# Both down projections by seven block products, with the weight sums moved

## The chip, the cores and the metric

The kernel runs on one core of a Trainium2 chip. The core has five engines that run side by side, each with its own queue of instructions in order: TensorE (PE in the profile, its weight loads PEld), VectorE (DVE), ScalarE (ACT), GpSimd (POOL) and SyncE (SP), which issues most of the DMA transfers. Sixteen DMA engines move the data. The metric is the time of one execution on the device in microseconds, lower is better, as the median of several runs.

## The reference

One decoder layer on 512 tokens of width 1024, in float32:

```python
h = swiglu(rms_norm(x, ffn1_pre_norm), ffn1_w_gate, ffn1_w_up, ffn1_w_down)
x = x + 0.5 * rms_norm(h, ffn1_post_norm)
u = rms_norm(x, mix_pre_norm)
# mixer: u @ w_in, three branches (sparse attention, gated delta rule,
# cross-attention into 256 memory tokens), each to width 1024, gated by
# sigmoid(u @ w_branch_gate), summed, then @ w_out
x = x + rms_norm(merged @ w_out, mix_post_norm)
h = swiglu(rms_norm(x, ffn2_pre_norm), ffn2_w_gate, ffn2_w_up, ffn2_w_down)
x = x + 0.5 * rms_norm(h, ffn2_post_norm)

def swiglu(x, w_gate, w_up, w_down):
    return (jax.nn.silu(x @ w_gate) * (x @ w_up)) @ w_down
```

The hidden width of both feed-forward blocks is 2816 = 22 x 128. The two products with `w_down` (512 x 2816 by 2816 x 1024) are what the change is about.

## The kernel before

**Products in three matmuls.** Every float32 operand of a large product is split into a rounded high part and a remainder, hi and lo. ScalarE makes hi (a cast), VectorE or POOL makes lo (a subtraction). A product of a 128-row block is then three matmuls, hi·hi, lo·hi and hi·lo, accumulated in PSUM (`mm3`, lines 115 to 119). Weights come in tiles of 128x512 through `wload` (line 88), from a small ring of buffers: SyncE issues the load of `wraw`, ScalarE casts to `whi`, VectorE subtracts to `wlo`; where `pool_every` is set, every so many-th subtraction goes to POOL instead.

**Stages.** In order of time: first gate and up projections, 22 tiles of 128 hidden features, result in `H` (features by tokens); first down projection; norm, then the input projections, the delta rule and the compression of the mixer; attention (task list `order2`); the gated merge of the branches (task list `order4`); `w_out`; the second gate and up; the second down; the last norm and store.

**Products by seven.** A two-by-two block product can be made with seven block products instead of eight when sums of the blocks of both operands are formed first (Winograd's form of Strassen's scheme). The kernel before does that in four places. From the seventh tile on, both gate and up stages pair the gate and up weights of a tile with two halves of the input (`fast_prods`, line 425; `fast_load` forms the weight sums on VectorE). The gated merge does the same with two gate tiles. And the second down projection does it (`down7`, line 535), with token halves and halves of the hidden features as blocks: 11 feature tiles, two token blocks of 128 and 512 output columns to a product.

The weight sums of `down7` are too large for VectorE. `weight_sums` (line 518) forms them in DRAM, by DMA from POOL: four tensors `T1` to `T4`, each made by a copy and one accumulating transfer, eight transfers in all, each cut into four pieces of 704 KB. A piece is issued after the matmul that was last when the piece was written (`self.order(i, self.mmark, Sync)`): POOL's queue stands until PE has done it. In the kernel before the 32 pieces are for the second down projection (`ffn2_d`), and they are issued beside the *first* gate and up stage, two in each of the sixteen tiles by seven.

**The first down projection before** is the plain one (`down_half`, line 505): for each half of the tokens and each half of the output columns, 22 feature tiles times two token blocks times three matmuls. `hsplit` makes hi and lo of `H`, tile by tile. Around it stands a list of tasks, `order0`: `d0`, `d1` are the two token halves of the projection, `p` its norm and residual (`postnorm`), `n` the next norm, `t` the transposes that give the input of the mixer (`xth`, `xtl`), `k0` to `k3` and `v` the key and value projections of the memory tokens, which depend on nothing here and fill PE while a norm runs. The norm of the memory tokens (`mem_norm`) is made during `d0`.

**What sets the order.** The program is written task by task; a planner then orders the instructions of each engine by priority, which is the place in the program unless a task is moved ahead by its number in `off0`, `off`. An engine never reorders on the chip: an instruction that waits holds up everything behind it on its engine. The plan is by `tasks` and the lists in `PRM`.

**In `down7` before** the seven products come in the order X = first block, Q (`T3`), X again (`T2`), Y, Z (`T1`), X again (`T4`), Z again. X, Y, Z and Q are two PSUM banks each, all eight together. Between them stand copies from bank to bank (X to Y, X to Z), Q to SBUF, and the sums of the output for the last 256 tokens in `c2`. In the last product the last eight feature tiles are done for the first token block, then for the second, so that the ending of the first block runs beside it.

Of the kernel before, what the change touches and what calls it, by code (L numbers as in the profile page):

```python
# [15 lines left out]
OP = mybir.AluOpType  # L16
# [23 lines left out]
class Body:  # L40
    def __init__(self, ctx, tc, a, out, tap):
        self.tc, self.nc, self.a, self.out, self.tap = tc, tc.nc, a, out, tap
        pool = lambda name, **k: ctx.enter_context(tc.tile_pool(name=name, **k))
        self.sp = pool("sp", bufs=2)
        self.cp = pool("cp", bufs=1)
        self.ring, self.ringi = None, 0
        self.nload, self.pool_every = 0, 0
        self.tp = pool("tp", bufs=2)
        self.wp = pool("wp", bufs=1)
        self.wx, self.nx = None, 0  # L50
        self.ps = pool("ps", bufs=1, space=bass.MemoryType.PSUM)
# [18 lines left out]
        self.dmaq = 0  # L70
        self.own = 0


    def bank(self, tag, name):
# [40 lines left out]
    def mm3(self, out, lh, ll, rh, rl, first, last):  # L115
        t = self.nc.tensor
        t.matmul(out, lh, rh, start=first, stop=False)  # L117
        t.matmul(out, ll, rh, start=False, stop=False)  # L118
        self.mmark = t.matmul(out, lh, rl, start=False, stop=last)  # L119
# [299 lines left out]
    def fast_tile(self, f, S, T, banks, s7, H, side=()):  # L419
        g, up = self.fast_prods(S, T, banks, s7, side=side)  # L420
# [4 lines left out]
    def fast_prods(self, S, T, banks, s7, mid=(), side=()):  # L425

        nc, v, te = self.nc, self.nc.vector, self.nc.tensor
        hi, lo = S
        a, q7, g, u = banks
        a, q7, u = a[:, :256], q7[:, :256], u[:, :256]  # L430

        def prod(out, w, t, start=False):
            th, tl = T[t]
            for k in range(4):
                c = slice(k * P, k * P + P)
                wh, wl = hi[:, w, c], lo[:, w, c]
                m = lambda x, y, **kw: te.matmul(out, x, y, skip_group_check=True, **kw)  # L437
                m(wh, th[:, k], start=start and k == 0, stop=False)
                m(wl, th[:, k], start=False, stop=False)
                self.mmark = m(wh, tl[:, k], start=False, stop=k == 3)  # L440
            if side and w in (self.S_S3, self.S_S1):
                side.pop(0)()
# [1322 lines left out]
```

## Time and profile before

| | us |
|---|---|
| median of 3 runs | 1324.87 |
| the three runs | 1321.78, 1324.87, 1331.35 |
| the profiled execution, its own time | 1321.78 |
| its span, first to last instruction | 1320.0 |
| first gate and up, tiles by seven (they overlap the last plain tiles) | 69.6 to 248.5 |
| first down projection with its memory work | 248.5 to about 398 |
| attention | about 640 to 800 |
| gated merge | about 800 to 930 |
| second gate and up, tiles by seven | about 1056 to 1207 |
| second down projection | 1207.4 to 1312.4 |
| ending after the last matmul | 1312.4 to 1320.0 |

The profile is one execution, and the times in its rows are from the start of its span. A row of the windows view gives the length of a stretch, then for each engine how long it was busy in it (and with how many instructions), the clock granted to TensorE as a share of full speed, the mean busy share of the sixteen DMA engines and the GB/s that they moved. A row of a group view gives line, engine, operation, output and inputs with their shapes and count, then total busy time and the mean of one in ns, then how long the engine sat idle just before them and for whom. Matmuls overlap in the pipeline: a matmul's own span is longer than the distance to the next.

### The profile page before, as it was taken

Reading aid. Unit: us, or ns where it says so; the run is one execution under the profiler, and the core shown is the slowest. Engines: PE = TensorE matmul, PEld = TensorE weight load, DVE = VectorE, ACT = ScalarE, POOL = GpSimd, SP = SyncE. Lnnn points to the kernel's source line nnn. Section 1 sums busy time; section 2 is a strip of 40 time slices with the busy share of each in tenths; the row PEclk is TensorE's granted clock in tenths of the full one; section 3 lists DMA queues with packets and bytes.
Section 4 is the critical chain, followed back from the end, with each engine's and each line's share of the span. In section 5 each row is a group of like instructions: output and inputs, shape, how many; then the busy total and the mean of one; then the engine's idle time right before and its main releaser. Section 6 shows DMA issues by size and latency. Waiting matters only on the chain. (4 is left out here: it accounts for less than half of the span.)

```text
span 1320.0 us, 21997 instructions
## 1 busy us (share of the span) xinstructions
PE 1286.8 (97%) x8025; PEld 1118.4 (85%) x8025; DVE 968.8 (73%) x1812; ACT 735.7 (56%) x1532; POOL 151.7 (11%) x145
## 2 busy tenths in 40 slices
PE   9999999999999989999999999999999999999997
PEld 7889999877888778888777778898878899999886
DVE  6898778478575876754779776565699687876977
ACT  7566555476555644323655545543678466664653
POOL 0021111100000321110221112132300000000000
PEclk9999999999999999999999999999999999999999
DMA  7557998877664433241321133232854533323763
GB/s 253 193 184 259 232 239 239 193 247 225 219 207 133 119 104 91 58 144 45 117 65 50 48 106 110 73 97 65 287 165 147 176 113 113 112 82 105 263 206 137
DMA packets 113165, 198.52 MB, mean 150 GB/s; under 512 B 18604, under 2 KB 28192, under 8 KB 113056
## 3 DMA queue, kind: packets, MB, share of 16 engines
q1 hardware_dynamic: 103808, 173.78, 41.3%
q0 software_dynamic: 8960, 23.07, 7.8%
q8 instruction: 63, 1.03, 0.3%
q14 instruction: 46, 0.38, 0.1%
q10 hardware_dynamic: 288, 0.26, 0.1%
HBM read 187.03 MB, written 33.08 MB: 167 GB/s over the span
## 5 line engine op out<-in xcount | busy, mean ns | idle before, releaser
L106 ACT CAST whi<-wraw 128x512 fp32r<-128x512 f32 (+1 forms) x286 | 173.7, 617 | 159.2 <-PE pfm L119 59.7
L109 DVE TENSOR_TENSOR wlo<-wraw,whi 128x512 fp32r<-128x512 f32 (+1 forms) x255 | 174.8, 694 | 74.9 <-ACT whi L106 65.7
L117 PE MATMUL pfm<-xth,whi 128*128 128x512 f32 x272 | 108.0, 402 | 1.0 <-DVE X L1055 0.6
L118 PE MATMUL pfm<-xth,wlo 128*128 128x512 f32 x272 | 108.4, 403 | 0.1
L119 PE MATMUL pfm<-xtl,whi 128*128 128x512 f32 x272 | 107.8, 402 | 0.0
L437 PE MATMUL smm<-thi,fset 128*128 128x256 f32 x384 | 68.9, 278 | 4.3 <-ACT ss L450 4.3
L109 POOL TENSOR_TENSOR wlo<-wraw,whi 128x512 fp32r<-128x512 f32 x28 | 38.0, 1356 | 229.1 <-ACT whi L106 165.0
L437 PEld LDWEIGHTS smm<-thi,fset 128*128 128x128 f32 x384 | 58.3, 188 | 4.8 <-ACT ss L450 4.7
L117 PEld LDWEIGHTS pfm<-xth,whi 128*128 128x128 f32 x272 | 51.0, 189 | 11.6 <-issue 1.8
L459 DVE TENSOR_TENSOR up<-s,smm 128x256 f32<-128x256 f32 x32 | 13.5, 421 | 62.5 <-ACT se L454 62.5
L119 PEld LDWEIGHTS pfm<-xtl,whi 128*128 128x128 f32 x272 | 50.9, 188 | 9.7 <-issue 0.8
L118 PEld LDWEIGHTS pfm<-xth,wlo 128*128 128x128 f32 x272 | 50.9, 188 | 9.2 <-DVE wlo L109 0.5
L437 PE MATMUL smm<-thi,fxtl 128*128 128x256 f32 x192 | 53.5, 279 | 0.6 <-DVE fxtl L412 0.6
L437 PE MATMUL smm<-thi,fxth 128*128 128x256 f32 x192 | 53.4, 278 | 0.2 <-ACT ss L450 0.2
L584 ACT CAST ringh<-ringr 128x1024 fp32r<-128x1024 f32 (+1 forms) x39 | 37.8, 975 | 27.3 <-PE acc_s L597 6.5
L437 PE MATMUL se<-thi,fset 128*128 128x256 f32 x256 | 45.7, 278 | 0.0
L403 DVE TENSOR_TENSOR fs<-fq 128x1024 f32<-128x1024 f32 x32 | 39.0, 1219 | 8.3 <-issue 5.4
L1173 ACT ACTIVATE Pm<-Pm,nm 128x384 f32<-128x384 f32 (+2 forms) x64 | 35.6, 558 | 14.5 <-DVE nm L1172 13.9
L437 PEld LDWEIGHTS se<-thi,fset 128*128 128x128 f32 x256 | 38.8, 188 | 0.0
L437 PEld LDWEIGHTS smm<-thi,fxtl 128*128 128x128 f32 x192 | 36.1, 188 | 1.0 <-DVE fxtl L412 1.0
L409 ACT CAST fset<-fq 128x512 fp32r<-128x512 f32 x48 | 29.6, 620 | 12.5 <-PE ss L437 5.9
L437 PEld LDWEIGHTS smm<-thi,fxth 128*128 128x128 f32 x192 | 36.0, 188 | 0.4 <-ACT ss L450 0.4
(645 smaller groups left out, 4271.7 us busy)
## 6 DMA issues: line engine op xcount, KB each, us to landing
wraw<-in_ffn_d_dram SPq DMA_DIRECT2D x94, 256.0 KB, 2.9
T<-in_ffn_d_dram POOLq DMA_DIRECT2D x24, 704.0 KB, 8.3
fq<-in_ffn_g_dram SPq DMA_DIRECT2D x64, 256.0 KB, 3.0
fq<-in_ffn_u_dram SPq DMA_DIRECT2D x64, 256.0 KB, 3.8
ringr<-T SPq DMA_DIRECT2D x20, 512.0 KB, 4.1
wraw<-in_ffn_g_dram SPq DMA_DIRECT2D x34, 256.0 KB, 3.2
wraw<-in_ffn_u_dram SPq DMA_DIRECT2D x34, 256.0 KB, 3.4
woraw<-in_w_out_dram SPq DMA_DIRECT2D x32, 256.0 KB, 4.2
```

The source lines that it names most:

```text
L106: nc.scalar.copy(hi, raw)
L109: eng.tensor_tensor(lo, raw, hi.bitcast(F32), op=OP.subtract)
L117: t.matmul(out, lh, rh, start=first, stop=False)
L118: t.matmul(out, ll, rh, start=False, stop=False)
L119: self.mmark = t.matmul(out, lh, rl, start=False, stop=last)
L403: add = lambda *x: v.tensor_tensor(*x, op=OP.add)
L409: nc.scalar.copy(hi[:, i], q[:, i])
L437: m = lambda x, y, **kw: te.matmul(out, x, y, skip_group_check=True, **kw)
L459: v.tensor_tensor(up[:, 256:], s7, a, op=OP.subtract)
L584: nc.scalar.copy(hi, raw)
L1173: nc.scalar.activation(pm, pm, AF.Exp, bias=nm[:, qb : qb + 1], scale=-1.0, accum_out=sm[:, qb : qb + 1])
```

## The change

The first down projection is made by `down7` too. Its weight sums take the place of the second one's beside the first gate and up stage, in 8 x 11 = 88 pieces of 256 KB, and the second one's, still in 32 pieces of 704 KB, go beside attention and the gated merge. Pieces are no longer issued at fixed places in a tile but by a count of matmul columns: `tick` is called once per group of three matmuls, adds their columns, and when the sum passes `pace` (4600 and 15000) the next piece is issued, waiting for that matmul. The counting starts at the fourth tile of the first stage, and at the first task of attention. Three-matmul groups of `mm3` and of `fast_prods` count; the other matmuls of attention do not.

```diff
+    def tick(self, ins, cols):
+        self.mmark = ins
+        if self.side:
+            self.cols += cols
+            if self.cols >= self.pace:
+                self.cols -= self.pace
+                self.side.pop(0)()
...
-    def weight_sums(self, w, n):
+    def weight_sums(self, w, n, cuts, pace):
...
-        r = nh * P // 8
-        return T, [... for s in todo for j in range(4)]
+        r = nh * P * 512 // 1024 // cuts
+        self.pace, self.cols = pace, 0
+        self.side = [lambda s=s, c=slice(r * j, r * j + r): piece(*s, c) for s in todo for j in range(cuts)]
+        return T
...
+                T1 = self.weight_sums("ffn1_d", 1, 11, 4600)
...
-                self.T2, side = self.weight_sums("ffn2_d", 2)
-                self.fast_phase(1, 4, xh, xl, RB, H, step, side)
+                self.fast_phase(1, 4, xh, xl, RB, H, step)
...
                     self.pool_every = 2
+                    T2 = self.weight_sums("ffn2_d", 2, 4, 15000)
                     self.tasks(task, PRM["order2"], "M")
```

In `down7` the order of the products changes for both projections: Y moves from fourth to sixth, so that the output of tokens 256 to 511 (`c2`) is complete after the fifth product and not the sixth. Z follows directly on the copy from X; to cover that copy, the last two weight groups of the third product (four feature tiles) are done for the first token block, then the copy of its bank is issued, then the second token block. Within a pair of feature tiles the token blocks are now the outer loop.

```diff
         seq = (
-            (X, d[0, :nh], part(0, 0), True),
-            (Q, T[2], s3, True),
-            (X, T[1], s2, False),
-            (Y, d[0, nh:], part(0, 1), False),
-            (Z, T[0], part(1, 0), False),
-            (X, T[3], part(1, 1), False),
-            (Z, d[1, nh:], s4, False),
+            (X, d[0, :nh], part(0, 0), True, end1, 0),
+            (Q, T[2], s3, True, end7, 0),
+            (X, T[1], s2, False, end6, 2),
+            (Z, T[0], part(1, 0), False, end5, 0),
+            (X, T[3], part(1, 1), False, end4, 0),
+            (Y, d[0, nh:], part(0, 1), False, None, 0),
+            (Z, d[1, nh:], s4, False, None, 4),
         )
...
-                if m == 5:
+                if m == 4:
                     for i in range(2):
                         self.ending([self.c2[:, 0, i], self.c2[:, 1, i]], x, gb, 2 + i, self.out, tmp)
```

The first projection has its own homes: weights of the first six feature tiles of the first product and of the last two products come by `wload` (tiles of 128x512), the others in pairs through a ring made of `xth` and `xtl`, with three pairs of buffers for the remainders (the second projection has six). The tasks hang on the products: the memory norm after the second product (`m == 1`), gain and residual after the third, `p2`, `n1`, `t1` (norm, next norm and transposes of tokens 256 to 511) after the fifth, the memory keys 0 and 1 after the sixth, the rest after the last.

```diff
-'order0': ['d0', 'p0', 'n0', 't0', 'd1', 'k2', 'k0', 'p2', 'p3', 'n1', 'v', 'k3', 'k1', 't1']
+'order0': {4: ['p2', 'n1', 't1'], 5: ['k0', 'k1'], 6: ['p0', 'p1', 'k2', 'n0', 'v', 'k3', 't0']}
...
+            def done(m):
+                nonlocal x, uh, ul
+                if m == 1:
+                    mem.extend(self.mem_norm(self.mmark, ("o", "r")))
+                if m == 2:
+                    self.gain7("ffn1_post", 0.5, gb)
+                    x = self.load_x(a["x"], after=self.mmark)
+                if m == 4:
+                    uh, ul = self.xt()
+                self.tasks(task, PRM["order0"].get(m, ()), key="0")
+                self.pool_every = 0
...
+            self.down7(H, "ffn1_d", T1, banks, done, lambda m, k: m and m < 5 or not m and k > 5, [x[:, i] for x in lor for i in range(2)][:3])
...
-            self.down7(H, "ffn2_d", self.T2, x1, banks, done)
+            self.down7(H, "ffn2_d", T2, banks, done, lambda m, k: m or k > 5)
```

More of the change, by code (lines that the diff above doesn't have):

```diff
@@ L118, in mm3 @@
         t.matmul(out, ll, rh, start=False, stop=False)
-        self.mmark = t.matmul(out, lh, rl, start=False, stop=last)
+        self.tick(t.matmul(out, lh, rl, start=False, stop=last), 3 * math.prod(out.shape[1:]))
+    def tick(self, ins, cols):
[5 more added lines that the diff above has]
+                self.side.pop(0)()
     def split(self, hi, lo, src):
@@ L478, in fast_phase @@
             i = f % 2
[L479 removed]
+            self.fast_tile(f, self.sets[i], T, banks[i], s7[i], H)
             if f + 2 < FT:
@@ L530, in piece, with down7_homes, down7_banks, down7_ring @@
             self.order(i, self.mmark, mybir.DependencyClass.Sync)
-        r = nh * P // 8
-        return T, [lambda s=s, c=slice(r * j, r * j + r): piece(*s, c) for s in todo for j in range(4)]
-    def down7(self, H, w, T, x1, banks, done):
+        r = nh * P * 512 // 1024 // cuts
+        self.pace, self.cols = pace, 0
+        self.side = [lambda s=s, c=slice(r * j, r * j + r): piece(*s, c) for s in todo for j in range(cuts)]
+        return T
+    def down7_homes(self, n, x1, lors):
+        pool = lambda name: x1.enter_context(self.tc.tile_pool(name=f"{name}{n}", bufs=1))
+        dw = pool("dw")
+        gb = dw.tile([P, 2, 512], F32, name="gb")
+        self.sraw = [dw.tile([P, 4, 256], F32, name=f"sraw{i}") for i in range(2)]
+        self.q7 = dw.tile([P, 2, 512], F32, name="q7")
+        self.c2 = dw.tile([P, 2, 2, 512], F32, name="c2")
+        lor = [dw.tile([P, 2, 512], F32R, name=f"lor{i}") for i in range(lors)]
+        self.wx = None
+        if lors < 4:
+            self.wx = pool("wy")
+            self.own = 6
+        dv = pool("dv")
+        ch = lambda nm: dv.tile([P, 4, 256], F32R, name=nm)
+        sh2, sh3, sl2, sl3 = (ch(x) for x in ("sh2", "sh3", "sl2", "sl3"))
+        if lors == 4:
+            dv.tile([P, 128], F32, name="gap")
+        dv = pool("dz")
+        sl0, sl1, sh0, sh1 = (ch(x) for x in ("sl0", "sl1", "sh0", "sh1"))
+        self.sring = [sh0, sh1, sh2, sh3], [sl0, sl1, sl2, sl3]
+        return gb, lor
+    def down7_banks(self):
+        b4, c4 = self.bank8()
+        return b4[:2], c4[:2], c4[2:], b4[2:]
+    def down7_ring(self, los):
+        rings = [self.cp.tile([P, KT, SEQ], t, tag=g, name=n) for t, g, n in ((F32, "xth", "ringr"), (F32R, "xtl", "ringh"))]
+        two = lambda x: [x[:, i : i + 2] for i in range(0, x.shape[1], 2)]
+        self.wring = two(rings[0]), two(rings[1]), los
+    def down7(self, H, w, T, banks, done, ringed, lor=()):
         nc, v = self.nc, self.nc.vector
@@ L574, in down7, with weights @@
         wr, wh_, wl_ = self.wring
-        def weights(m, src, k):
+        def weights(m, src, ks, lo):
             nonlocal wslot
-            if m == 0 and k < 6:
-                return {k: self.wload(src[k])}
-            n = 2 if (nh - k) % 2 == 0 else 1
+            if not ringed(m, ks[0]):
+                return {ks[0]: self.wload(src[ks[0]], lo=lo)}
+            n, k = len(ks), ks[0]
             raw, hi, lo = wr[wslot % len(wr)][:, :n], wh_[wslot % len(wh_)][:, :n], wl_[wslot % len(wl_)][:, :n]
@@ L586, in weights @@
             return {k + i: (hi[:, i], lo[:, i]) for i in range(n)}
-        for m, (acc, src, make, start) in enumerate(seq):
-            ops, ws = {}, {}
+        for m, (acc, src, make, start, end, lag) in enumerate(seq):
+            ops, ws, groups, k = {}, {}, [], 0
+            while k < nh:
+                n = 2 if ringed(m, k) and (nh - k) % 2 == 0 else 1
+                groups.append(list(range(k, k + n)))
+                k += n
             cuts = (0, 1, 4, 8, nh) if m == 0 else (0, 4, 8, nh)
-            lag = 8 if m == 6 else 0
+            lo = list(lor) if lag and not ringed(m, nh - 1) else []
+            hold = len(groups) - lag
             def mm(i, k):
@@ L647, in xt, with gain7, mem_norm @@
                 self.cp.tile([P, KT, SEQ], F32R, tag="xtl", name="xtl"))
-    def mem_norm(self, after=None):
+    def gain7(self, name, f, gb):
+        i = self.nc.sync.dma_start(gb.rearrange("p h d -> p (h d)"), self.a[name].partition_broadcast(P))
+        self.order(i, self.mmark)
+        for h in range(2):
+            self.nc.vector.tensor_scalar(gb[:, h], gb[:, h], f * (1, -1)[h], None, op0=OP.mult)
+    def mem_norm(self, after=None, tags=("e",)):
         mh = self.cp.tile([P, KT, NMEM], F32R, tag="mth", name="mth")
```

152 lines of the change are left out of this document (60 added, 92 removed).

## The prediction

> **What bounds the kernel now.** I read the page's busy table first, then the chain of waits, then the windows stage by stage, then the groups by shape and the waits inside the stages that change.
>
> ```profile
> span 1320.0 us, 21997 instructions
> PE 1286.8 (97%) x8025; PEld 1118.4 (85%) x8025; DVE 968.8 (73%) x1812; ACT 735.7 (56%) x1532; POOL 151.7 (11%) x145
> ```
>
> PE is the bound, so an engine that is late matters only where PE stands. But 97% is a union of overlapping spans: what a matmul costs is the distance to the next, and the chain gives that.
>
> ```profile
> 1059.91 1.36 PE smm L437 x12
> ...
> 1252.47 14.96 PE acc_e L597 x66
> ```
>
> Twelve matmuls of 256 columns follow each other in 1.36 us (2259 columns per us), 66 of 512 columns in 14.96 us (0.2267 us each, not the 0.39 of the busy time). One block product of a down projection is 11 k-blocks x 2 token blocks x 3 matmuls = 66, so 14.96 us. The first down projection is the plain one:
>
> ```profile
> L117 PE MATMUL acc_e<-whi,Hh 128*128 128x512 f32 x44 | 17.3, 394 | 0.0
> ...
> 248.50:285.00 36.50, 32.88 (x147) 25.63 (x147) 28.18 (x65) 26.26 (x60) 0.00 (x0) 1.00 0.81 244
> 285.00:315.20 30.20, 30.20 (x135) 25.00 (x134) 22.48 (x44) 21.30 (x49) 0.00 (x0) 1.00 0.77 235
> 315.20:348.20 33.00, 32.28 (x149) 26.23 (x148) 25.55 (x60) 22.11 (x44) 2.08 (x4) 1.00 0.76 243
> 348.20:381.30 33.10, 33.10 (x158) 27.50 (x157) 17.65 (x35) 15.90 (x31) 0.00 (x0) 1.00 0.62 188
> ...
> 1207.40:1222.50 15.10, 15.10 (x68) 12.41 (x67) 14.45 (x17) 10.75 (x16) 0.00 (x0) 1.00 0.75 250
> 1222.50:1237.50 15.00, 15.00 (x68) 12.43 (x67) 15.00 (x15) 9.86 (x12) 0.00 (x0) 1.00 0.62 195
> 1237.50:1252.50 15.00, 15.00 (x68) 12.43 (x67) 14.52 (x16) 10.88 (x15) 0.00 (x0) 1.00 0.88 325
> 1252.50:1267.40 14.90, 14.90 (x67) 12.33 (x67) 12.34 (x14) 8.97 (x11) 0.00 (x0) 1.00 0.78 262
> ```
>
> Columns: length, then PE, PEld, DVE, ACT and POOL busy, clock, DMA share, GB/s. The four windows from 248.5 are the four quarters of the plain projection (44 matmuls in each of twelve such groups: 528). PE loses 3.62 + 0.72 = 4.3 us there. The four from 1207.4 are the first products of the second projection, already by seven: PE loses nothing, with VectorE busy 56.3 of 60.0 us.
>
> **The change part by part.** I sum against the profiled execution: 1321.78 us (span 1320.0). It is the lowest of the three runs, 3.1 under the median of 1324.87; I add 3.1 at the end.
>
> *The product saved.* 528 matmuls become 7 x 66 = 462: 66 x 0.2267 = **-15.0 us**, all on PE, which nothing else there can fill. Half as many DMA issues for the weights that come in pairs, 77 k-blocks for 88; nothing here is dearer on SyncE.
>
> *VectorE in the first down projection.* It must now form the sums of the activations.
>
> ```profile
> L109 DVE TENSOR_TENSOR wlo<-wraw,whi 128x512 fp32r<-128x512 f32 x98 | 66.9, 689 | 32.2 <-ACT whi L106 28.8 <-PE acc_s L119 1.2 <-PE acc_e L119 0.7
> L123 DVE TENSOR_TENSOR Hl<-H,Hh 128x256 fp32r<-128x256 f32 x44 | 17.6, 419 | 2.3 <-ACT Hh L122 2.1
> L204 DVE SCALAR_TENSOR_TENSOR mtl<-ptr,gpre,mth 128x256 fp32r<-128x256 f32 x8 | 3.5, 475 | 0.1
> ...
> L585 DVE TENSOR_TENSOR lor<-ringr,ringh 128x1024 fp32r<-128x1024 f32 x20 | 24.2, 1217 | 2.1 <-ACT ringh L584 2.1
> L609 DVE TENSOR_TENSOR sl<-H,sh 128x1024 fp32r<-128x1024 f32 x11 | 13.4, 1216 | 0.1
> L554 DVE SCALAR_TENSOR_TENSOR H<-H 128x1024 f32<-128x1024 f32 x2 | 2.4, 1214 | 0.0
> ```
>
> Out: 88 weight remainders x 0.689 + 44 operand remainders x 0.419 = 79.0 us. In, per product: five pairs x 1.217 + one single of 0.689 = 6.8, operands 2.75 x 1.216 = 3.3, together 10.1; seven make 70.8; the operand sums add four passes (one for S3, two for S2, one for S4) of 2.75 x 1.214 = 13.4, and four end sums of 128x512 at 0.689 add 2.8: 87.0. So VectorE gains 8 us of work while PE loses 15: from 93.9 of 132.8 us (the four windows) to about 102 of 118, 71% to 86%. It bunches: the second projection's first four products already take 56.3 of 60 us, and the memory norm joins them here (3.5 us of mtl, an estimated 6 with its scaling). What waits for that is the queue of weight remainders, three pairs deep here (six there), and behind it PE.
>
> Old stalls of 4.3 us go. For the new ones the rows bound me: none (VectorE at 97% from 1207.4) to about 14 (3.6 us, as in 248.5, at each of the four places where extra work is queued: memory norm, tokens 2-3, tokens 0-1, next stage). I take 6, nearer the row of this very stage with the memory norm in it: **+1.7** (-4.3 to +9.7).
>
> *Its tail.* After the last product only k2, v and k3 cover tokens 0-1 (two of the four key projections move ahead of the product).
>
> ```profile
> 381.30 0.40 PE L119 MATMUL acc_s<-lor,Hh 128*128 128x512 f32 x1
> 381.53 0.28 PE L117 MATMUL pfm<-mth,whi 128*128 128x256 f32 x1
> ...
> 384.39 0.40 PE L117 MATMUL pmv<-whi,mth 128*128 128x512 f32 x1
> ...
> 395.24 0.39 PE L119 MATMUL pmv<-wlo,mth 128*128 128x512 f32 x1
> ...
> 396.67 1.33 ACT L188 ACTIVATE xb<-xb,rny 128x512 f32<-128x512 f32 x2
> ```
>
> Cover: 384.39 - 381.53 = 2.9 for a key projection, 11.2 for v, so 17.0 us. The chain to hide, last matmul to normed x, ran 381.3 to 398.0 here: 16.7 us. Even, with the transposes' evictions open; they are in the 6.
>
> *Order of the products.* Z is now read right after it is copied from X. Held-back matmuls cover the first copy; the second has three matmuls (0.68 us) before PE needs it.
>
> ```profile
> L624 ACT COPY acc_s<-acc_mm 128x512 f32<-128x512 f32 x2 | 1.2, 578 | 0.5 <-PE acc_mm L597 0.5
> ```
>
> 0.58 us plus hand-overs, and perhaps a 1.0 us weight cast ahead of it on ScalarE: **+0.5** for both projections (0.2 to 2.4). The earlier ending of tokens 2-3 in the second one hides under full PE rows: 0; uncovered it would be its own VectorE work, some 7 us.
>
> *First gate and up stage.* The same 23 MB of sums, now 88 pieces of 256 KB every 4600 / 2259 = 2.04 us from the fourth tile on, 179 us; before, 32 pieces of 704 KB over 157 us (89.3 to 246.2).
>
> ```profile
> 129.00:170.00 41.00, 39.11 (x338) 38.91 (x338) 30.98 (x36) 23.59 (x48) 7.56 (x8) 1.00 1.03 228
> 170.00:191.00 21.00, 18.63 (x163) 18.43 (x162) 14.72 (x18) 11.19 (x24) 2.40 (x4) 1.00 0.89 264
> 191.00:211.00 20.00, 19.75 (x172) 19.55 (x171) 15.66 (x19) 11.97 (x26) 3.81 (x4) 1.00 1.01 230
> ...
> 1065.60:1207.00 141.40, 141.40 (x1242) 141.40 (x1241) 105.08 (x125) 81.34 (x168) 0.00 (x0) 1.00 0.28 90
> ...
> L529 POOL DMA_DIRECT2D T<-in_ffn_d_dram x24: 582/936/988, 89.3 to 246.2; - x24
> T<-in_ffn_d_dram POOLq DMA_DIRECT2D x24, 704.0 KB, 8.3
> wraw<-in_ffn_d_dram SPq DMA_DIRECT2D x94, 256.0 KB, 2.9
> ```
>
> PE loses 4.5 us where the DMA share is at 0.9 to 1.03 with accumulating pieces, and none in the same loop without them (0.28). The flow falls to 157/179 = 88%, and a weight load stands behind 256 KB, not 704. A third of the loss staying, **-3.0** (-4.5 to +2, if the fourth to sixth tiles, loading weights one at a time, suffer instead). Issuing takes POOL 88 x 0.6 to 0.99 us = 53 to 87 of 179; only the gates' row scaling queues there.
> The Trainium skill (DMA: Bandwidth & Descriptors, "Measured (HBM→SBUF, 128 partitions, SWDGE, issued from GpSimd)") says to batch transfers to 1 MiB or more; by the fit it gives in "Anatomy of one DMA", 88 pieces take 229 us against 117 for 32 (an estimate), which speaks against the smaller pieces if they run one after another. By it 50 us of pieces would spill past the stage, and the sum be 2.7 us (rival 4's price for 50 us) and the 3.0 not gained higher, -8.6. This trace has 8.3 us for a piece that the fit puts at 3.7, beside other traffic.
>
> *Attention.* 32 pieces of 704 KB, one per 15000 / 2259 = 6.6 us of counted matmuls: by the code's order 13 before the gated pairs, 19 beside them. Each waits on POOL for its matmul and then issues (0.94).
>
> ```profile
> 640.00:800.00 160.00, 158.90 (x858) 120.96 (x857) 125.64 (x338) 85.23 (x223) 25.01 (x19) 1.00 0.24 75
> 800.00:930.00 130.00, 128.58 (x848) 114.81 (x847) 78.78 (x110) 63.73 (x139) 35.13 (x22) 1.00 0.25 80
> ...
> L109 POOL TENSOR_TENSOR wlo<-wraw,whi 128x512 fp32r<-128x512 f32 x28 | 38.0, 1356 | 229.1 <-ACT whi L106 165.0 <-issue 56.2 <-DVE cs L1116 4.3
> ```
>
> Behind them on POOL stand the weight remainders (PE waits for those) and the merges. DMA has room (0.25, plus 704 KB per 6.6 us). Nothing leaves this stage, so no gain. **+1.5**; at most 8: the 4.5 us that all pieces cost beside the first stage, and one or two remainders late by 0.94 + 1.36 = 2.3.
>
> Sum: -15.0 + 1.7 + 0.5 - 3.0 + 1.5 = -14.3. Profiled execution 1307.5, median **1310.6 us**. Every term at its end: -21.6 to +7.1.
>
> **The rivals.**
> 1. *VectorE becomes the bound of the first down projection.* For: 56.3 of 60 us before the memory norm is added, three pairs of lead instead of six. Against: 86% over the stage. Stalls of 14, not 6: 1318.6.
> 2. *Nothing new stalls.* The down stage runs as the second one does, the sums cost nothing: -21.6, 1303.3. For: the full rows from 1207.4. Against: 3.6 us lost at 248.5.
> 3. *Slower: POOL's queue in attention.* A piece is placed ahead of a remainder and waits for a matmul of the product before; PE then waits 2.3 us. Six hits eat the 14.3 us, twelve make it slower by 1%. With 16 of 32: -14.3 - 1.5 + 36.8, so 1345.9. Against: POOL's remainders wait for ScalarE's cast 165 us in all; POOL is idle when they come.
> The Trainium skill (SBUF — State Buffer, the section "SBUF: two separate sides") says a VectorE copy locks POOL out of writing descriptors, 3.1 us for 0.62; by it 16 hits would cost 71 us and the time be 1380 (an estimate). The issues' maximum of 0.988 us, with VectorE busy 30.98 of 41, disagrees.
> 4. *Small pieces back up.* Landed one at a time at the 2.9 us of the nearest 256 KB row, 88 need 255 us; 76 spill past the stage. At the 4.5 us per 82 lost where the share is about 1, 4.2 us, and the 3.0 not gained: 1317.8. Against: pieces are issued without waiting for each other, but for the same rows eleven pieces back.
> 5. *The change does not do what it says*: the weights' sums come so late that the fifth product waits 15 us for them. Its last piece is issued 13,000 columns (6 us) before the stage ends, the product starts 60 us after; it would have to land 80 us late. Then the time stays at 1325.
>
> **How the numbers follow.** Forecast, within 4 us of 1310.6: 0.52. Rivals 1 to 5: 0.16, 0.14, 0.08, 0.07, 0.03. One per cent, about what a measurement can tell from no change, is 13.2 us: the bound lies at 1311.6, a little above the forecast. Faster takes 0.34 of the forecast's 0.52 and rival 2: 0.48. Same takes its other 0.18, rivals 1, 4 and 5: 0.44. Slower is rival 3: 0.08. The range, 1302 to 1322, holds the forecast and rivals 1, 2 and 4 and leaves out rival 3, rival 5 and the far ends.
>
> **What would show it.** Right: 66 matmuls fewer; seven groups of 66 in about 105 us plus the work between them; PE gaps in the gate and up loop under 2 us; POOL issues near 0.6 us for 256 KB. Wrong in the second term: PE waiting there for lor or wlo with VectorE over 95%. Wrong in the last: PE in 640 to 930 waiting for POOL wlo with a T issue just before it. Wrong altogether: PE waiting for ringr from T at the second to fifth product.

## The result, and the profile after

| | before | after |
|---|---|---|
| median of 12 runs, us | 1322.72 | 1312.40 |
| lowest and highest, us | 1316.74, 1331.35 | 1310.15, 1321.75 |
| the profiled execution: its time, its span | 1321.78, 1320.0 | 1313.67, 1311.9 |

The ratio is 0.9929, with a 95% interval of 0.9908 to 0.9951: about 9.4 us faster, which is less than the one per cent that the prediction took as the bound. The busy table of the page after the change:

```profile
span 1311.9 us, 21823 instructions
PE 1272.6 (97%) x7959; PEld 1104.9 (84%) x7959; DVE 985.1 (75%) x1774; ACT 733.5 (56%) x1483; POOL 207.3 (16%) x233
```

There are 66 matmuls fewer (8025 to 7959), and POOL has 88 instructions more, which are the pieces of the first projection. Cutting both profiled executions at the same matmuls tells where the 8.1 us of span went (each row is the time between first matmuls of two stages):

| stage | before | after | difference |
|---|---|---|---|
| start to the first matmul of the first down projection | 249.0 | 247.8 | -1.2 |
| from there to the first `ptm` (mixer's input) | 151.9 | 139.4 | -12.5 |
| mixer, to the first `ps` | 240.3 | 240.9 | +0.6 |
| attention and gated merge, to the first matmul of `w_out` | 292.0 | 296.0 | +4.0 |
| `w_out` and the first plain tiles of the second gate and up | 98.3 | 99.3 | +1.0 |
| second gate and up from there: last plain tiles, tiles by seven | 175.7 | 175.7 | 0.0 |
| second down projection and ending | 112.8 | 112.8 | 0.0 |

The windows of the kernel after: the four quarters of the down stage, three windows of the first gate and up, then attention and the merge, which are cut at the same matmuls as further windows below (columns: length, then PE, PEld, DVE, ACT and POOL busy, clock, DMA share, GB/s):

```profile
247.80:282.60 34.80, 34.80 (x155) 28.72 (x154) 33.61 (x35) 27.18 (x37) 0.00 (x0) 1.00 0.76 254
282.60:317.40 34.80, 32.25 (x149) 26.04 (x149) 32.72 (x51) 25.41 (x36) 0.00 (x0) 1.00 0.83 291
317.40:352.20 34.80, 34.58 (x180) 29.22 (x179) 28.66 (x58) 22.58 (x44) 2.08 (x4) 1.00 0.42 134
352.20:387.20 35.00, 32.57 (x169) 26.79 (x168) 24.83 (x67) 21.48 (x45) 1.36 (x3) 1.00 0.72 229
129.00:170.00 41.00, 38.38 (x320) 37.98 (x320) 29.35 (x35) 22.85 (x47) 11.73 (x18) 0.96 0.88 219
170.00:191.00 21.00, 21.00 (x187) 21.00 (x186) 17.29 (x21) 12.49 (x26) 7.72 (x11) 1.00 0.91 212
191.00:211.00 20.00, 19.33 (x170) 19.13 (x169) 15.43 (x19) 11.77 (x24) 6.04 (x10) 1.00 0.96 249
628.10:760.51 132.41, 130.69 (x724) 96.22 (x722) 107.92 (x308) 70.65 (x192) 27.52 (x25) 1.00 0.37 106
760.51:924.07 163.56, 160.84 (x992) 141.24 (x991) 103.91 (x143) 81.66 (x175) 56.23 (x47) 1.00 0.72 185
```

Attention and the merge in the kernel before, at the same matmuls:

```profile
641.20:770.88 129.68, 128.94 (x724) 96.41 (x722) 104.71 (x308) 70.11 (x192) 21.13 (x16) 1.00 0.19 58
770.88:933.20 162.32, 160.54 (x991) 141.04 (x991) 101.95 (x143) 81.75 (x175) 40.16 (x26) 1.00 0.31 99
```

In the down stage VectorE is busy 119.8 of 139.4 us, 86%. TensorE stands still five times there, and a sixth time just behind the first `ptm`, where the table already counts the mixer. These are the rows behind the gaps in TensorE's timeline, with the idle time and its releaser in brackets:

```profile
295.10 0.50 PE L658 MATMUL acc_s<-lor,sh 128*128 128x512 f32 x1 [0.96 <-DVE lor L641]
303.07 0.73 PE L208 MATMUL ptr<-cst,xm 128*128 128x128 f32 x5 [1.59 <-DVE mtl L213]
372.29 0.50 PE L119 MATMUL pmv<-wlo,mth 128*128 128x512 f32 x1 [0.54 <-DVE wlo L109]
374.72 0.50 PE L117 MATMUL pmv<-whi,mth 128*128 128x512 f32 x1 [1.47 <-ACT mkv L727]
387.18 0.53 PE L117 MATMUL ptm<-whi,xth 128*128 128x288 f32 x2 [0.41 <-ACT xth L212]
392.95 0.37 PE L117 MATMUL ptm<-whi,xth 128*128 128x288 f32 x1 [1.76 <-DVE xtl L213]
```

The first two, 2.6 us, are at the memory norm; the other four, 4.2 us, are behind the last product. Of the four the first two, 2.0 us, are waits inside the value projection of the memory tokens (a weight remainder, a copy out of PSUM), the last two, 2.2 us, are for the transposes' evictions on ScalarE and VectorE. The second copy of the new order, X to Z, leaves no gap of its own in either projection. POOL's groups and the landing times of the pieces:

```profile
L536 POOL DMA_DIRECT2D T<-in_ffn_d_dram x90 | 67.6, 751 | 198.8 <-PE pg L119 38.7
L109 POOL TENSOR_TENSOR wlo<-wraw,whi 128x512 fp32r<-128x512 f32 x28 | 38.8, 1388 | 112.5 <-ACT whi L106 98.1
...
T<-in_ffn_d_dram POOLq DMA_DIRECT2D x66, 256.0 KB, 5.8
T<-in_ffn_d_dram POOLq DMA_DIRECT2D x24, 704.0 KB, 7.4
```

A piece of 256 KB lands in 5.8 us, not in the 2.9 that a weight load of that size took in the kernel before, and one is issued every two microseconds: they overlap. The last of the 88 is issued at 242.8 and lands at 247.9, as the down projection starts: nothing spills.

### The profile page after: what moved, and what is told of

It reads as the page before. It is cut to its first block, busy times and chain, and to the rows that moved or that the text cites. A ratio compares the mean times of both kernels' runs of the same rounds, so it can differ in the third digit from the quotient of the medians.

```text
span 1311.9 us, 21823 instructions
## 1 busy us (share of the span) xinstructions
PE 1272.6 (97%) x7959; PEld 1104.9 (84%) x7959; DVE 985.1 (75%) x1774; ACT 733.5 (56%) x1483; POOL 207.3 (16%) x233
## 5 line engine op out<-in xcount | busy, mean ns | idle before, releaser
L106 ACT CAST whi<-wraw 128x512 fp32r<-128x512 f32 (+1 forms) x226 | 136.2, 616 | 135.2 <-PE pfm L119 51.3
L109 DVE TENSOR_TENSOR wlo<-wraw,whi 128x512 fp32r<-128x512 f32 (+1 forms) x195 | 136.3, 709 | 49.5 <-ACT whi L106 48.1
L536 POOL DMA_DIRECT2D T<-in_ffn_d_dram x90 | 67.6, 751 | 198.8 <-PE pg L119 38.7
L640 ACT CAST ringh<-ringr 128x1024 fp32r<-128x1024 f32 (+1 forms) x66 | 63.6, 973 | 33.5 <-PE acc_mm L658 9.1
L641 DVE TENSOR_TENSOR lor<-ringr,ringh 128x1024 fp32r<-128x1024 f32 (+1 forms) x54 | 59.2, 1106 | 3.2 <-ACT ringh L640 2.4
L1234 ACT ACTIVATE Pm<-Pm,nm 128x384 f32<-128x384 f32 (+2 forms) x64 | 35.6, 558 | 15.0 <-DVE nm L1233 14.3
L671 DVE TENSOR_TENSOR sl<-H,sh 128x1024 fp32r<-128x1024 f32 (+2 forms) x38 | 41.1, 1083 | 3.7 <-ACT sh L670 3.7
L658 PE MATMUL acc_mm<-ringh,sl 128*128 128x512 f32 x108 | 42.0, 389 | 0.0
```

Source lines behind the costliest of these rows:

```text
L106: nc.scalar.copy(hi, raw)
L109: eng.tensor_tensor(lo, raw, hi.bitcast(F32), op=OP.subtract)
L536: i = g.dma_start(o[c], x[c], max_dma_last_dim=2048, **({"accum_op": OP.add} if add else {}))
L640: nc.scalar.copy(hi, raw)
L641: tt(lo, raw, hi.bitcast(F32), op=OP.subtract)
L658: e = lambda a, b, s, f: nc.tensor.matmul(acc[i], a, b, start=s, stop=f, skip_group_check=True)
```

## The experiments

Beside each run's median stands what the trace of one execution shows by stage. Code that two kernels share is as good as a repetition: the down stage after the change took 138.9 to 143.7 us in nine executions (mean 140.5), and the seven tile pairs of the first gate and up stage (in the kernel after from 97.6 to 238.5 us) beside 88 pieces took 136.4 to 141.8 us in ten (mean 139.0). Attention and merge scatter far less, under 2 us over seven executions.

The scatter of the down stage has a cause that the traces show. In some executions the clock granted to TensorE falls to 0.50 for 3.41 us, as here, behind a stall at the memory norm in the run without the second projection's pieces (the second row is the same length of time right after it):

```profile
307.85:311.26 3.41, 3.41 (x10) 2.63 (x9) 3.41 (x6) 2.56 (x5) 0.00 (x0) 0.50 0.78 255
311.30:314.71 3.41, 3.41 (x16) 2.81 (x16) 1.57 (x4) 1.79 (x2) 0.00 (x0) 1.00 0.97 354
```

Ten matmuls instead of sixteen. The five executions whose down stage holds no such stretch took 138.9 to 139.8 us, the three with one 141.0 to 141.8, the one with two 143.7. So before a difference of two or three microseconds in one execution is put down to an edit, the granted clock of the stage has to be looked at.

### What the pieces cost attention and merge

**Without them.**

```diff
-                    T2 = self.weight_sums("ffn2_d", 2, 4, 15000)
+                    T2, self.side = T1, []
```

> The 32 weight-sum pieces of the second projection are left out of the attention and merge stages (the second down projection reads the first one's sums in their place, so the last outputs are other numbers; matmuls, transfers and sizes there stay). The time between the first po matmul of attention and the end of the last merge grew by about 4 us with the pieces (a lead of 13.1 us at 644 became 9.1 at 932). Theory, the pieces cost that: the lead of 13 us over the kernel before is kept to the end, about 4 us faster than the changed kernel, ratio to before about 0.990. Rival, the two stages lost it by something else that came with the shift (buffers, the state left by the earlier stages): the lead still shrinks to 9 us and the time does not move by more than 1 us. Without pieces the planner also puts the attention's matmuls in the order of the kernel before, so a gain here does not yet say whether order, queue or traffic is the cause; the next two runs do.

Median 1309.23 us, ratio 0.9899 (0.9871 to 0.9927). The stage took 290.1 us, where the seven executions with pieces took 294.7 to 296.6 (mean 295.7). The loss is theirs, and larger than against the kernel before (292.0): 5.6 us.

**Small ones.**

```diff
-        self.side = [lambda s=s, c=slice(r * j, r * j + r): piece(*s, c) for s in todo for j in range(cuts)]
+        self.side = [lambda s=s, c=slice(r * j, r * j + r // part): piece(*s, c) for s in todo for j in range(cuts)]
...
-                    T2 = self.weight_sums("ffn2_d", 2, 4, 15000)
+                    self.weight_sums("ffn2_d", 2, 4, 15000, 16)
+                    T2 = T1
```

> The same 32 pieces in attention, with the same waits on GpSimd and the planner's order of the changed kernel, but each moves a sixteenth of its rows (the second projection reads the first one's sums, so the last outputs are other numbers). Theory, traffic: about 4 us faster than the changed kernel, as without the pieces. Rival, GpSimd's queue or the planner's order: no faster than the changed kernel by more than 1 us, and the lead falls from 13 to 9 us between 644 and 932 as before.

1311.10 us, 0.9914 (0.9888 to 0.9939); the stage took 293.1 us. The windows of attention and of the merge, from the same matmul to the same matmul as those of the kernel after; first without pieces, then with small ones:

```profile
632.97:762.70 129.73, 128.99 (x724) 96.44 (x722) 104.77 (x308) 70.23 (x192) 21.17 (x16) 1.00 0.19 58
762.70:923.11 160.41, 160.17 (x991) 141.09 (x991) 101.28 (x143) 82.01 (x175) 39.87 (x26) 1.00 0.31 99
```

```profile
628.78:761.04 132.26, 130.59 (x723) 96.26 (x721) 107.67 (x308) 70.69 (x192) 26.55 (x25) 1.00 0.20 60
761.04:921.92 160.88, 160.41 (x992) 141.17 (x991) 101.24 (x143) 82.08 (x175) 53.68 (x47) 1.00 0.35 105
```

The two halves lose for different reasons. The merge takes 163.56 us with full pieces, 160.88 with small ones, 160.41 without: its loss is traffic, at a DMA share of 0.72. Attention takes 132.41, 132.26 and 129.73: small pieces cost it as much as full ones, although its DMA share is then that of no pieces at all (0.20 and 0.19). So 2.7 us come from what the added instructions in POOL's queue bring with them. One thing is the plan: in the traces the order of TensorE's rows in the two stages differs between the kernel after and the run without pieces in 70 places, 61 of them in attention, while the kernel before has the order of the run without pieces, and 129.68 us. Another is the time of the issues (a copy takes 0.71 us even for a small piece). No run told them apart. TensorE's gaps over 0.5 us in attention wait for the softmax on VectorE, none for a weight remainder of POOL, which speaks for the order; they are only part of the 2.7 us:

```profile
661.07 0.74 PE L1231 MATMUL ps<-KA,qa 128*128 128x512 f32 x2 [0.61 <-DVE nm L1233]
...
714.27 0.66 PE L1253 MATMUL ppt<-cst,Pm 128*128 128x128 f32 x2 [0.81 <-DVE Pm L229]
```

(These two rows are of the kernel after; the kernel before has one such gap, of 0.74 us.)

**Without the wait.**

```diff
-            self.order(i, self.mmark, mybir.DependencyClass.Sync)
+            self.order(i, self.mmark, how)
...
-                    T2 = self.weight_sums("ffn2_d", 2, 4, 15000)
+                    T2 = self.weight_sums("ffn2_d", 2, 4, 15000, mybir.DependencyClass.NoSync)
```

> The full 32 pieces, at the same places in GpSimd's queue but for six rows, and the planner's order of the changed kernel on every other engine; only the semaphore wait of each piece for its matmul is gone, so that a piece goes out as soon as GpSimd reaches it. Theory of the prediction's third rival, the wait holds GpSimd's weight remainders behind it: 2 to 4 us faster than the changed kernel in 644 to 932. Rival, traffic or order: within 1 us of the changed kernel.

1323.53 us, 1.0004 (0.9985 to 1.0024): the whole gain of the change is gone, 11 us. The stage took 303.9 us. The two largest gaps of TensorE in its merge:

```profile
799.38 0.80 PE L446 MATMUL de<-uhi,mset 128*128 128x256 f32 x2 [2.50 <-ACT do L457]
...
876.08 0.38 PE L446 MATMUL de<-xth,mset 128*128 128x256 f32 x1 [2.81 <-DVE mset L421]
```

Neither outcome had been expected. TensorE's order is that of the kernel after, but the pieces now go out in pairs within a microsecond or so, and the second of these gaps waits for the sums of the gate weights. At both gaps the granted clock also falls to 0.50 for 3.41 us. The wait on POOL, which the prediction's third rival had as the cost, is what paces the traffic.

**Ahead of attention.**

```diff
             odh = self.cp.tile([P, 4, SEQ], F32R, tag="mth", name="odh")
+            T2 = self.weight_sums("ffn2_d", 2, 4, 6000)
...
-                    T2 = self.weight_sums("ffn2_d", 2, 4, 15000)
```

> The second projection's 32 pieces are moved ahead, beside the mixer (one per 6000 columns of its counted matmuls, from 400 us on, done before attention); attention and merges then stand in the planner's order without pieces. If the mixer, where TensorE idles 6 of 120 us and the DMA rings are a third busy, takes them for nothing, attention and merges give back 5.4 us and the time is 5 us under the changed kernel's. Rival: the mixer's chains run through GpSimd, and a piece that waits there for its matmul and is issued in 0.6 to 0.8 us holds them up; 32 times 0.8 us would be 25 us, and any loss over 5.4 makes it slower than the changed kernel.

1341.60 us, 1.0152 (1.0119 to 1.0185). Attention and merge took 289.9 us, as without pieces, and the mixer 273.9 instead of 240.9. Two of its windows, then the largest of TensorE's gaps in the first of them and the POOL row ahead of it:

```profile
400.00:440.00 40.00, 30.66 (x150) 24.59 (x149) 21.66 (x58) 17.87 (x40) 12.96 (x16) 0.93 0.89 263
440.00:480.00 40.00, 33.51 (x150) 27.45 (x149) 27.19 (x61) 19.02 (x45) 13.79 (x17) 0.86 1.05 255
...
437.30 0.79 PE L117 MATMUL pfm<-xth,whi 128*128 128x512 f32 x1 [7.31 <-ACT whi L106]
...
431.26 1.05 POOL L878 TENSOR_TENSOR dec<-rowsb,gbt 128x512 f32<-128x512 f32 x1 [9.93 <-DMA rowsb<-drows]
```

The rings, 0.40 and 0.37 busy there without pieces, are full (0.89 and 1.05), and the mixer's own small transfers and weights come late; the wait of POOL named here is for a DMA. During and behind TensorE's four longest waits (27.4 us together) the granted clock is 0.50 for 30.7 us in all. TensorE was busy for 19.4 of these, so up to 9.7 of the 33 us are the clock (an estimate: half of 19.4). A loss of the size that the rival had came, but the rows show waits and clock, not issues; the planner's order differs here too, and no run separates it from the traffic.

**Behind the merge.** The pieces stand beside `w_out` and the second gate and up stage.

```diff
                     self.tap("mg", mg)
+                    T2 = self.weight_sums("ffn2_d", 2, 4, 17500)
```

> The second projection's 32 pieces are moved out of attention and merges to the output projection and the second gate and up stage, one per 17500 columns (7.7 us) from 924 us on. The planner then orders attention as without pieces. Theory, order and traffic cost attention and merges 5 to 6 us, and a stage with the DMA rings 0.3 busy takes half-rate pieces for 1 us or less: 4 us faster than the changed kernel, ratio to before about 0.990. Rival, the second gate and up stage loses as the first one does beside its pieces, 0.1 us a piece and more: no faster than the changed kernel.

1312.96 us, 0.9921 (0.9894 to 0.9948): no faster, as the rival had it. Attention and merge took 289.9 us, but `w_out` and the plain tiles 103.0 instead of 99.3, and the loop 179.2 instead of 175.7. At one per 7.7 us, beside a loop whose own DMA share is 0.3, the 32 pieces cost 7.1 us.

### What the pieces cost the first gate and up stage

**Without them.** The projection reads `d[0, 11:]` and three more blocks of its weight in place of `T1`.

> The 88 pieces of the first projection are left out (it reads four plain blocks of its weight in place of the sums, so every output behind it is other numbers). Theory, the pieces still saturate the DMA rings beside the first gate and up stage: TensorE's gaps there, 4.1 us from 89 to 211, go to under 1 us, 3 to 4 us faster than the changed kernel at the first matmul of the down projection. Rival, the gaps belong to the stage's own weight loads: within 1 us.

The first matmul of the down projection came 7.4 us earlier, and the seven tile pairs took 134.0 us, where ten executions with the pieces took 139.0 in the mean. The seven pairs in one window each: the kernel before, the kernel after, and this run.

```profile
96.90:238.78 141.88, 137.37 (x1177) 136.78 (x1176) 105.65 (x123) 79.51 (x163) 21.58 (x28) 1.00 0.89 234
97.56:238.45 140.89, 136.76 (x1177) 135.97 (x1176) 105.97 (x123) 79.59 (x163) 46.19 (x65) 0.99 0.91 216
97.01:231.01 134.00, 134.00 (x1177) 134.00 (x1176) 105.27 (x123) 79.80 (x163) 0.00 (x0) 1.00 0.31 97
```

Without pieces TensorE never stands still. Of the 5.0 us that the 88 pieces cost in the mean, 2.6 are idle time (0.3 to 5.1 in the ten executions). In the other 2.4 TensorE is busy, but its matmuls follow each other more slowly: in seven of the ten a part of the loop runs at the slower rate of the last section, and two, that of the kernel after among them, hold a stretch at half clock.

The time of the run, 1312.97 us, 0.9918 (0.9890 to 0.9946), does not show the gain. Its profiled execution lost 4.9 us again in the second gate and up loop, for which see the last section, and 2.7 in the mixer, where the clock was halved twice; its other five executions have no trace.

**Larger ones.**

```diff
-                T1 = self.weight_sums("ffn1_d", 1, 11, 4600)
+                T1 = self.weight_sums("ffn1_d", 1, 4, 12650)
```

> The first projection's sums again in 32 pieces of 704 KB, spread over the same stretch (one per 12650 columns). Theory, what counts is the traffic and not the size of a piece: the seven tile pairs from 118 to 240 take as long as with 88 pieces, 137.7 to 141.2 us in four executions so far. Rival, the prediction's term (small pieces let the weight loads through): 3 us longer than with 88.

1313.96 us, 0.9928 (0.9904 to 0.9951); the seven pairs took 138.1 us, 3.5 of them idle, both inside the spread of the 88 pieces. The size of a piece makes no difference that one execution can show.

**The second part of the change alone**, in the kernel before: its 32 pieces leave the first stage for attention and merge, and the first down projection stays plain.

> The kernel before with one part of the change alone: the second projection's 32 pieces leave the first gate and up stage and go to attention and merges, one per 15000 columns; the first down projection stays plain. By the runs so far: the seven tile pairs of the first gate and up stage, 141.9 us before, go to the 134.0 they take without pieces (138.4 if the loop falls into its slower matmul rate), and attention with merges goes from 292.0 to 295.5. So 4.5 us faster than before (1 to 5), ratio 0.9966. Rival, the old 32 pieces had cost that stage little and the difference was the rate alone: 1 us faster to 3 us slower.

1319.65 us, 0.9967 (0.9942 to 0.9992): 3.6 us faster, about as expected. The seven pairs took 134.0 us (141.9 with the pieces), the stage up to the down projection 242.6 (249.0), attention and merge 296.5 (292.0). The plain down stage took 149.9, two less than in the kernel before, where its first weights (`whi`) had come 2.0 us late.

### What VectorE costs the first down projection

**The memory norm one product later.**

```diff
-                if m == 1:
+                if m == 2:
                     mem.extend(self.mem_norm(self.mmark, ("o", "r")))
-                if m == 2:
+                if m == 3:
                     self.gain7("ffn1_post", 0.5, gb)
```

> The memory norm is queued after the third product of the first down projection instead of the second, the post gain and the load of x after the fourth instead of the third; nothing else moves. Theory, VectorE is full where the activation sums of the third product and the memory norm come together: TensorE's gaps of 0.96 and 1.59 us at 294 and 301 go, and 1.5 to 2.5 us of the stage with them. Rival, VectorE's total is what counts (86% busy): the gaps only move to the next products, and the stage from the first down matmul to the first ptm stays within 0.7 us of 139.4.

1312.99 us, 0.9922 (0.9894 to 0.9950): no faster. The stage took 143.0 us, but with two stretches at half clock in it, as many as the execution of 143.7, so this time does not decide for the rival. TensorE's gaps up to the memory norm's end add up to 2.9 us, where the kernel after has 2.6: they moved, and did not go.

**Both moves**, this one and the pieces behind the merge:

> Both moves together: the second projection's pieces beside output projection and second gate and up stage, and the memory norm one product later. Theory, they add up, since they lie in different stages: 5.5 to 8 us faster than the changed kernel, about 1305.5. Rival, one of the two gives nothing: 2 to 4 us.

1312.57 us, 0.9918 (0.9891 to 0.9945): no faster than the changed kernel, which neither the theory nor the rival had. What attention gave back went to the stages that took the pieces. The down stage, without a stretch at half clock, took 138.3 us, 0.6 below the lowest of the unmoved ones. The gaps at the memory norm had moved and shrunk to 1.8 us:

```profile
292.42 0.49 PE L658 MATMUL acc_s<-lor,sh 128*128 128x512 f32 x1 [0.61 <-DVE lor L641]
...
304.31 0.44 PE L208 MATMUL ptr<-cst,xm 128*128 128x128 f32 x2 [1.15 <-DVE xm L196]
```

**Without the activation sums.**

```diff
+        if w == "ffn1_d":
+            s3, s2, s4 = part(0, 0), part(0, 0), part(0, 0)
```

> In the first down projection the four passes of VectorE that form the sums of the activations are left out (the plain blocks are multiplied in their place, so every output behind it is other numbers): 13 us less VectorE work, the same matmuls, loads and casts, the memory norm where it was. The changed kernel idles TensorE six times in that stage, 0.96 and 1.59 us at the memory norm (294, 301) and 0.54, 1.47, 0.40 and 1.77 us behind the last product (372 to 391), 6.7 us in all. Theory, VectorE full around the third product is the cause of the first two: they go to under 0.6 together, the stage (first down matmul to first ptm, 138.9 to 143.7 us in nine executions) takes 137 or less, and the four behind the last product stay. Rival, the memory norm's own chain is the cause: 1.5 us or more stay there.

1309.20 us, 0.9913 (0.9887 to 0.9939); the stage took 137.2 us, without a stretch at half clock, 1.7 under the lowest of the nine executions with the sums. What is left at the memory norm, and two of the gaps behind the last product:

```profile
287.74 0.44 PE L208 MATMUL ptr<-cst,xm 128*128 128x128 f32 x2 [0.62 <-DVE xm L196]
...
367.49 0.50 PE L119 MATMUL pmv<-wlo,mth 128*128 128x512 f32 x1 [0.54 <-DVE wlo L109]
...
369.91 0.50 PE L117 MATMUL pmv<-whi,mth 128*128 128x512 f32 x1 [1.45 <-ACT mkv L729]
```

VectorE's load is the cause at the memory norm: 2.6 us became 0.6, a hair over what the theory had asked for. Behind the last product nothing changed.

### The rate of a loop

> In the second gate and up stage the first matmul of seven tiles waits for ScalarE's silu of the tile before, so that TensorE stalls about a microsecond every second tile; nothing else changes. Theory, a loop of 256-column matmuls keeps one of two rates (0.1133 or 0.1178 us each, a pair of tiles in 19.16 or 19.79 us) and can change it only at a stall: both rates show between these stalls, each held from one stall to the next. Rival, the rate belongs to the execution (its data, buffers or clock): one rate throughout, whatever the stalls. The total is about 7 to 10 us longer.

A single execution, 1320.71 us, of which the stalls made 7. The first matmul after two successive stalls:

```profile
1065.97 0.50 PE L450 MATMUL smm<-thi,fset 128*128 128x256 f32 x2 [0.69 <-ACT sg L432]
...
1086.11 0.50 PE L450 MATMUL smm<-thi,fset 128*128 128x256 f32 x2 [0.69 <-ACT sg L432]
```

They are 20.14 us apart, and so were all the others: 19.16 and a stall. The loop kept the fast rate throughout. The theory's prediction failed, for stalls of 0.69 us in one execution.

## Why the prediction was right, and where it was wrong

The time, 1310.6 for 1312.4, was near and in the range. The saving was not: 14.3 us were forecast against the profiled execution, 8.1 came there and 10.3 between the medians. That the time came nearer than the saving is luck: the median of the kernel before, over 12 runs, is 2.1 us lower than over the three.

**The product saved and VectorE in the first down projection** were near. Forecast was -15.0 + 1.7, with half of the +0.5 for the copy -13.0; the profiled executions give -12.5, and the means of all executions, halved clock included, -10.4 (150.9 over two to 140.5 over nine). The new stalls were put at 6 and are 6.7, of which 1.8 stand in the row of the mixer; VectorE was put at 86% and is there. The reason given, the memory norm joining the fullest products, holds for 2.6 of the 6.7, as the run without the sums shows. Of the other 4.2, which no experiment touched, 2.2 are the transposes' evictions, which the prediction had left open within its 6. The last 2.0 are waits in the very work that was to cover the chain, which the step called "even" (cover of 17.0 against a chain of 16.7) did not count.

**The copy to Z** shows no cost of its own. A copy took 0.58 us, as forecast. Held-back matmuls covered the first. The second stood behind a weight cast, as the prediction feared, and ran from 293.78 to 294.36, under matmuls of the next weight group (six stood there, not three) and the wait for `lor` that ends at 295.10.

**The first gate and up stage** was to give 3.0 and gave 1.2 in the profiled pair, with a stretch at half clock in the execution after. On the mean of ten executions it gives 2.9 of the one execution before (139.0 to 141.9). So the size is not refuted, but what it was made of is another. The 4.5 us were TensorE's idle time in three windows; over the seven pairs the old pieces cost 7.9 us (141.9 against 134.0 without pieces), since the matmuls ran slower too, and 5.0 of these stay, not a third. Whether a smaller piece lets the weight loads through is open: idle time is 4.5 and 3.5 us in the two executions with large pieces and 0.3 to 5.1 in the ten with small ones. The Trainium skill (DMA: Bandwidth & Descriptors, "Measured (HBM→SBUF, 128 partitions, SWDGE, issued from GpSimd)") tells to batch, and by it small pieces should have been worse. These runs do not show it: 138.1 us with 32, 139.0 with 88. The 8.6 us that the prediction worked out by the page come close to the 8.1, but not for its reason, since the last piece lands as the stage ends and nothing spills.

**Attention** was the mis-sized term: +1.5 forecast, of a range to 8, and +4.0 measured (+3.7 on the mean). Its two named causes were traffic and late remainders. Traffic was one, 2.7 us in the merge. Late remainders were none. As much again, 2.7 us in attention, was not in the sum at all: it comes without traffic, and what differs there is the planner's order of work that did not change, in a stage from which "nothing leaves", and the issues on POOL. The wait, which looked like the risk, is what keeps the price down. Against the run without pieces the loss is 5.8 us; that only +4.0 show against the kernel before is because the merge was 1.9 us slower there than without pieces, though in the same order: TensorE waited there 1.40 us for VectorE at 897.26 and 0.36 for a weight remainder at 793.02, and the run without pieces has neither wait. Why is open.

**Not in the sum** were +0.6 in the mixer and +1.0 in `w_out`. The first row holds the gap of 1.76 us at 392.95, and is within what the mixer scatters (239.4 to 243.6; 239.4 to 240.9 where the clock was not halved in it). The second is in all executions of the new kernel, without pieces too (98.7 to 99.5 where the pieces do not stand there, against 98.3), and its cause is open.

**The rivals.** VectorE did not become the bound (6.7 us of stalls, not 14). Something did stall, so the second is out. Of the third, its mechanism is out where the change put the pieces: the trace shows no wait of TensorE for POOL's remainders in attention and merge, and without the wait on POOL the kernel is 11 us slower, not faster. The Trainium skill's rule (SBUF — State Buffer, "SBUF: two separate sides"), by which a VectorE copy would lock POOL out for 3.1 us at an issue, does not show here: no issue of the kernel after took over 0.99 us. The fourth and fifth did not come.

**The signs that were named.** 66 matmuls fewer came, and issues of 256 KB took 0.68 us in the mean. Gaps under 2 us in the gate and up loop did not come: 4.1 us. TensorE waited for `lor` once, 0.96 us, with VectorE busy for all of the 7 us around it (289 to 296): the sign against the second term showed, but only there. The low end of the sum, -21.6, does not follow from the ends given (-15.0 - 4.3 + 0.2 - 4.5 makes -23.6 with attention at nothing); nothing hung on it.

**The two parts.** Moving the second projection's pieces alone gave 3.6 us (0.9967). The first projection by seven with its own pieces accounts for the rest, 6.7 of the 10.3 us, each median taken against the kernel before of its own series: of 15.0 us of matmuls less than half is left after 5.0 beside gate and up and the new stalls.

## What to carry to other kernels

A saving on the bound engine is paid for where its preparation runs: price the traffic of the preparation in each stage by a window with it and one without, and do not expect it to vanish in a stage with idle rings (23 MB of sums cost 5.0, 5.6 and 7.1 us in three stages tried here, and 33 in the mixer, where they were packed closest). Instructions put into one engine's queue can reorder every other engine's work if a planner makes the order, so compare the order of the built program before putting a stage down as untouched. Before a wait is called a cost, look at what it paces. And read the granted clock of a stage before two executions of it are compared.

## What the runs showed of the hardware that was not expected

**Half clock behind short stalls.** Between the first 30 and the last 12 us of the 14 traces the clock granted to TensorE falls to 0.50 in 22 places, for 3.41 us each, in the mixer full of pieces also for 6.83 and 10.24. Each of them starts during a stall of TensorE of 1.46 us or more, or within 1.4 us of its end. Many such stalls are followed by none: the 1.76 us behind the first `ptm` never was. What decides between them the traces do not show. A stall of 1.5 us can thus cost nearly as much again (an estimate: the six matmuls missing above, at 0.2267 us each).

**Two rates.** The loops of 256-column matmuls run at one of two rates with no idle time and the same granted clock. The same two windows of the second gate and up stage, of the kernel after and of the run without the first projection's pieces:

```profile
1053.00:1100.00 47.00, 47.00 (x415) 47.00 (x414) 39.29 (x47) 29.66 (x61) 0.00 (x0) 1.00 0.35 114
1100.00:1150.00 50.00, 50.00 (x441) 50.00 (x440) 39.51 (x47) 31.11 (x64) 0.00 (x0) 1.00 0.37 116
```

```profile
1053.00:1100.00 47.00, 47.00 (x402) 47.00 (x401) 36.51 (x43) 28.60 (x58) 0.00 (x0) 1.00 0.34 112
1100.00:1150.00 50.00, 50.00 (x427) 50.00 (x426) 39.15 (x46) 29.82 (x61) 0.00 (x0) 1.00 0.34 106
```

415 against 402 matmuls in 47 us, 0.1133 against 0.117 us each; a pair of tiles takes 19.16 or 19.79 us. In the second loop a rate was kept from the first tile to the last, and the slow one, in 4 of the 14 profiled executions, costs 4.4 us over seven pairs. It fell on the profiled executions without `T1`, with both moves, with larger pieces and with the second part alone, and took back much of what three of them had gained. In the first loop, where stalls are of many lengths, eight of the twelve executions beside pieces ran a part of it at the slower rate, and the two without pieces none; equal stalls made on purpose in the second loop changed nothing. What sets it stays open. With it, 4 us in the time of one execution can be the rate alone, and a stage has to be compared with itself over several executions.
